# A fixed order for the first layer's drain, its memory attention and its attention loads, a new order at the entry, and other rooms for merged rows

## The chip, the cores and the metric

The kernel runs on one core of a Trainium2 chip. The metric is the device time of one execution in microseconds (us), lower is better. Times are medians of several runs; the profile is one execution of the same program, taken by the hardware profiler.

## The reference

Two layers of a decoder trunk work on 1024 tokens of width 1024, in float32. The first layer is dilated sliding-window attention, the second a gated linear recurrence; both also attend into 256 memory tokens. Only the first layer is touched. Cut to what matters:

```python
h = rms_norm(x, norm_gain[0])
cols = h @ w_in_a                      # q, k, v of 3 groups x 8 heads, memory queries, gate
mix = dilated_mixer(...)               # groups (window, dilation) = (128,1), (512,4), (2048,16)
    # per group: s = q k^T, masked softmax, o = p v; out also log of the denominator
    # o = sum over groups of softmax(lse)[g] * outs[g]      <- the "merge"
mem_out = memory_cross_attention(...)  # 4 heads: softmax(qm km^T) vm
y = concat([mix, mem_out]) * silu(gate)
x = x + y @ w_out
```

Every large product is done in TensorE passes on a split of the operands in a high and a low part (names ending in hi and lo, or h and l): high times high, low times high, high times low. The attention's own small products, s = q k^T and p v, run in float32 as they are.

## The kernel before, in words

Work is tiled by 128 tokens (NT = 8 tiles) and 128 x 512 results in PSUM, whose pools have few rooms: acc 3, s 2, pt (transposes) 2, po 1. Engines run their own queues in order; the order is set by a scheduler, except inside `pinned(...)`, which ties the instructions of the engines it names (TensorE alone when it names none) to the order in which the program writes them. Weights are loaded by SyncE (L204, into "raw" rooms), split by ScalarE (wh, L174 or L221) and VectorE (wl), some pieces ahead: `load_piece` issues a load, `split_piece` splits, `ahead(n)` does both until n pieces are ready.

The parts that the change touches come in this order:

- **Entry** (L1238 to L1297). Token tiles come in pairs j. A tile is scaled on VectorE (xt, L891), turned on TensorE (L896, into the two pt rooms), copied by ScalarE as the high part hhi and as r (L174), and VectorE makes the low part hlo (L910). Sums of a pair, s3, s2 and s4 (`x_sum`, L925), are split by `x_split`: ScalarE makes the high part (L174), GpSimd the low part (L931). In between, TensorE has gate matmuls (L1181 to L1183).
- **Drain of the projections** (L1375 to L1381). The last steps of the big projection are followed by eight steps k = 1 to 8 that finish heads on the other engines: turned heads are copied out of pt by ScalarE (L1113). TensorE runs 12 items of `memory_steps` in each, gate matmuls L591 at this point. Ahead of k = 3 and k = 4, `mem_turn` turns one tile of memory rows (16 transposes, L346, pt rooms; high and low part by ScalarE and VectorE, s3hi L174 and s3lo L324).
- **Memory attention** (L1466 to L1514). A pipeline over m = 0 to NT + 5: project memory queries (m < NT), norm them, turn them (L363), scores (L429 to L431), softmax on ScalarE and VectorE, turn (L458), values (L472 to L474, into po). In the last six steps the projection is over and the table `under` gives TensorE matmuls of a gate slice (L591; one slice has 48) to run between. Slices 0 to 3 of this gate are `MG0 = (0, 1)` and `MG1 = (2, 3)`; slice 1 is used up here.
- **Attention** (L1516 to L1661). Twelve heads in the order (2,0), (1,0), (2,1), (1,1), (0,0), (2,2), (1,2), (0,1), (2,3), (1,3), (0,2), (0,3), written (group, pair of heads); each has 8 steps m. A step gives scores of m (L1543), a turn of m - 2 (L1557) and values of m - 3 (L1570). Groups 1 and 2 write their results by ScalarE into a room of the pool "spill" (3 rooms, os) and from there to the scratch o_scr (`spill`, L1584 to L1592). Group 0 reads those back (og, L1528, two rooms a group), weighs them on GpSimd (L1612, L1613), and `merge` (L1617) adds its own part on VectorE (L1622) into a spill room and stores it. kT, qT and vv of the heads to come are loaded into two sets of rooms, one load a step. In group 2's heads each step also runs 3 matmuls L591 of slices 2 and 3. The attention is pinned on TensorE alone: SyncE's order is the scheduler's.

After the attention the kernel's order is the same in both versions.

## Time and profile before

| what | value |
|---|---|
| runs of the kernel | 2059.63, 2057.74, 2058.79 us; median 2058.79 us |
| the profiled execution's own time | 2058.84 us |
| its span in the profile | 2057.0 us, so 1.84 us lie around it |
| instructions | 29832, of them 10641 matmuls |
| TensorE (PE) busy | 2026.7 us (99%), 30.3 us idle |
| VectorE (DVE), ScalarE (ACT), GpSimd (POOL) busy | 1276.9, 887.1, 569.1 us |

In the profile PE is TensorE, PEld its weight loads, DVE VectorE, ACT ScalarE, POOL GpSimd and SP SyncE, which here issues DMA. L12 is line 12 of the kernel. A timeline row gives the start, the duration, engine, line, operation, `out<-in` and, in brackets, how long the engine had been idle before and what ended that. "granted clock" or PEclk is the share of TensorE's clock that was let through. The engine that is never idle sets the time, and that is TensorE: a change can only save what TensorE waits, or time that it runs slowed.

### The profile page before, as it was taken

The page shows a single profiled execution, that of the slowest core. Times are in us where ns is not written, and L with a number is a line of the kernel's source. Part 1 is how long each engine was busy: PE and PEld are TensorE (multiplying, and loading weights), DVE is VectorE, ACT ScalarE, POOL GpSimd, SP SyncE. Part 2 cuts the span into 40 slices and gives each one's busy share as a digit, 9 for nine tenths or more (in the row PEclk, how much of TensorE's full clock was granted, in tenths as well). Part 3 has the DMA queues.
Part 4 walks back from the last instruction along what each step waited for, and adds up shares of the span by engine and source line. Part 5 has one row for each costly group of instructions (what it writes and reads, how often), then busy time and mean ns, then how long its engine had stood idle before and what let it go on. Part 6 is the DMA issues. An engine that isn't in the chain of part 4 may idle for free.

```text
span 2057.0 us, 29832 instructions
## 1 busy us (share of the span) xinstructions
PE 2026.7 (99%) x10641; PEld 1720.2 (84%) x10641; DVE 1276.9 (62%) x2540; ACT 887.1 (43%) x1678; POOL 569.1 (28%) x690
## 2 busy tenths in 40 slices
PE   7999999999999999999999999999999999999999
PEld 6888888888888887888898888888888888888887
DVE  7745866736767356555567454484554888886543
ACT  6435555633554344546667332253364332232220
POOL 4105765703755046121123200070031000000221
PEclk9999999999999999999999999999999999999999
DMA  6445989553544426617998474524354111213643
GB/s 228 133 134 103 92 143 132 110 169 89 116 124 135 151 73 183 186 36 275 319 326 283 145 255 154 175 72 142 116 176 139 40 44 50 79 37 103 235 133 113
DMA packets 434339, 295.59 MB, mean 144 GB/s; under 512 B 221952, under 2 KB 350224, under 8 KB 434192
## 3 DMA queue, kind: packets, MB, share of 16 engines
q1 hardware_dynamic: 420992, 276.91, 48.1%
q10 hardware_dynamic: 13200, 16.78, 2.2%
q8 instruction: 85, 1.39, 0.3%
q14 instruction: 62, 0.51, 0.1%
HBM read 202.28 MB, written 91.36 MB: 143 GB/s over the span
## 4 chain that ended last, share of the span: by engine, by line
PE 50%; DMA 2%; ACT 1%; DVE 0%; issue 0%; POOL 0%; SPq 0%; ACTq 0%; DVEq 0%
PE acc L662 4%; PE acc L663 4%; PE acc L664 4%; PE acc L558 4%; PE acc L556 4%; PE acc L557 4%; PE s L1543 2%; PE acc L1997 2%; PE s L2142 2%; PE pt L2142 2%; PE acc L294 1%; PE acc L293 1%; PE acc L292 1%; PE pt L1557 1%; PE po L1570 1%; PE acc L1570 1%
## 5 line engine op out<-in xcount | busy, mean ns | idle before, releaser
L174 ACT ACTIVATE wh<-raw 128x1024 fp32r<-128x1024 f32 x207 | 217.2, 1054 | 185.0 <-PE acc L557 59.6
L975 DVE TENSOR_TENSOR wl<-raw,wh 128x1024 fp32r<-128x1024 f32 x136 | 169.2, 1244 | 120.0 <-ACT wh L174 119.4
L1089 POOL TENSOR_TENSOR rr<-rv,nhalf 128x4 f32<-128x4 f32 x96 | 121.5, 1266 | 391.5 <-DVE rv L1087 391.4
L183 POOL TENSOR_TENSOR rr<-rv,nhalf 128x4 f32<-128x4 f32 (+1 forms) x46 | 42.7, 930 | 608.2 <-DVE rv L181 581.8
L662 PE MATMUL acc<-wh,yhi 128*128 128x512 f32 x360 | 142.7, 399 | 0.5 <-ACT yhi L174 0.5
L1044 PE MATMUL acc<-wh,hhi 128*128 128x512 f32 x360 | 141.3, 393 | 0.0
L663 PE MATMUL acc<-wl,yhi 128*128 128x512 f32 x360 | 141.1, 392 | 0.0
L664 PE MATMUL acc<-wh,ylo 128*128 128x512 f32 x360 | 140.2, 394 | 0.0
L1046 PE MATMUL acc<-wh,hlo 128*128 128x512 f32 x360 | 140.2, 390 | 0.0
L1045 PE MATMUL acc<-wl,hhi 128*128 128x512 f32 x360 | 140.1, 389 | 0.0
L556 PE MATMUL acc<-hhi,wh 128*128 128x512 f32 x320 | 128.7, 402 | 0.0
L557 PE MATMUL acc<-hlo,wh 128*128 128x512 f32 x320 | 127.5, 399 | 0.0
L558 PE MATMUL acc<-hhi,wl 128*128 128x512 f32 x320 | 127.4, 398 | 0.0
L236 DVE TENSOR_TENSOR wl<-raw,wh 128x1024 fp32r<-128x1024 f32 x62 | 76.5, 1239 | 67.9 <-ACT wh L174 62.5
L979 DVE TENSOR_TENSOR raw<-raw 128x1024 f32<-128x1024 f32 x76 | 96.5, 1278 | 20.1 <-DMA raw<-in_w_in_a_dram 19.8
L1548 ACT ACTIVATE pa<-pa,st 128x128 f32<-128x128 f32 (+1 forms) x192 | 84.7, 443 | 45.9 <-DVE st L1546 45.4
L1546 DVE CUSTOM_DVE_ANT_0 pa<-s,masks 128x128 f32<-128x128 f32 (+1 forms) x192 | 59.6, 348 | 44.7 <-PE pt L1557 22.6
L674 DVE TENSOR_TENSOR x<-x,acc 128x512 f32<-128x512 f32 x62 | 42.2, 685 | 71.6 <-PE acc L664 71.5
L1543 PE MATMUL s<-kT,qT 128*128 128x128 f32 (+1 forms) x384 | 78.2, 326 | 1.9 <-DVE st L1546 1.1
L662 PEld LDWEIGHTS acc<-wh,yhi 128*128 128x128 f32 x360 | 67.7, 188 | 14.1 <-ACT yhi L174 0.8
L1046 PEld LDWEIGHTS acc<-wh,hlo 128*128 128x128 f32 x360 | 67.6, 188 | 14.2
L664 PEld LDWEIGHTS acc<-wh,ylo 128*128 128x128 f32 x360 | 67.6, 188 | 13.9
(477 smaller groups left out, 5685.4 us busy)
## 6 DMA issues: line engine op xcount, KB each, us to landing
raw<-in_w_in_a_dram SPq DMA_DIRECT2D x109, 512.0 KB, 4.3
raw<-in_w_in_b_dram SPq DMA_DIRECT2D x43, 512.0 KB, 3.9
qk_scr<-m SPq DMA_DIRECT2D x48, 256.0 KB, 3.9
kT<-qk_scr SPq DMA_DIRECT2D x24, 512.0 KB, 5.8
qT<-qk_scr SPq DMA_DIRECT2D x24, 512.0 KB, 7.3
vv<-v_scr SPq DMA_DIRECT2D x24, 512.0 KB, 5.5
o_scr<-os SPq DMA_DIRECT2D x96, 128.0 KB, 5.1
og<-o_scr SPq DMA_DIRECT2D x32, 256.0 KB, 4.8
```

What stands on the lines that cost most here:

```text
L174: A.activation(dst, src, AF.Copy)
L556: T.matmul(ps[:], wh[:, k, :], mh, start=k == 0, stop=False)
L557: T.matmul(ps[:], wh[:, k, :], ml, start=False, stop=False)
L558: T.matmul(ps[:], wl[:, k, :], mh, start=False, stop=k == 7)
L662: T.matmul(pss[ch][:], hi[:, k, :], wh[:, j, :], start=first and k == 0, stop=False)
L663: T.matmul(pss[ch][:], hi[:, k, :], wl[:, j, :], start=False, stop=False)
L664: T.matmul(pss[ch][:], lo[:, k, :], wh[:, j, :], start=False, stop=end and k == 3)
L975: V.tensor_tensor(lo[:], source(n, h), hi.bitcast(F32), op=OP.subtract)
L1044: T.matmul(flat, hi, wh, start=kt == 0 and p in (0, 1, 5), stop=False, **on)
L1045: T.matmul(flat, hi, wl, start=False, stop=False, **on)
L1046: T.matmul(flat, lo, wh, start=False, stop=kt == 3, **on)
L1089: G.tensor_tensor(r[:], sd[:], nhalf[:, :4], op=OP.pow)
```

## The change

- Entry, j = 0 only: the three `x_split` now come behind the copies and low part of the next tile (`x_high`, `x_keep`, `x_low` of tile 2) in place of ahead of them.
- Drain: `mem_turn(0)` comes behind step 3 (before: ahead of it), `mem_turn(1)` ahead of the fifth gate matmul of step 4 (before: ahead of step 4). A Tanh of one column (`A.activation(small.tile(...), nhalf[:, 0:1], AF.Tanh)`) is put ahead of step 1.
- Memory attention: slices 1, 2 and 3 form one stream, `cover`. `under` gives it 66 matmuls (before 48), and the attention's 32 steps of group 2 get the other 78: 2 each in the first 18, 3 each in the last 14 (before 3 in each). Weight pieces are loaded and split at written places, and the loads of the first head (`first_heads`) come one in each half step in place of all at once.
- Attention: SyncE is pinned too, so that loads and stores stand as the program writes them. `merge` takes every other room from the pool "gs" (2 rooms) and so has five in all with "spill". A weight piece is loaded and split at (1, 0) too (before: at odd pairs only).

```diff
                 x_sum(j, "s3")
                 x_sum(j, "s2")
-                x_split(j, "s3")
-                x_split(j, "s2")
-                if a_ and not j:
+                if j:
+                    x_split(j, "s3")
+                    x_split(j, "s2")
+                else:
                     x_scale(a_)
                 x_sum(j, "s4")
-                x_split(j, "s4")
+                if j:
+                    x_split(j, "s4")
...
                         x_low(a_, kh)
+                    if not j:
+                        for n in ("s3", "s2", "s4"):
+                            x_split(j, n)
...
         for k in range(1, BEHIND + 3):
             with pinned():
-                if k in (3, 4):
-                    mts.append(mem_turn(k - 3))
-                for _ in range(96 // (BEHIND + 2)):
+                if k == 1:
+                    A.activation(small.tile([128, 1], F32, name="ss1")[:], nhalf[:, 0:1], AF.Tanh)
+                for j in range(96 // (BEHIND + 2)):
+                    if (k, j) == (4, 4):
+                        mts.append(mem_turn(1))
                     next(ahead_of)
                 step(LAST + k, lambda: pieces(LAST + k))
+                if k == 3:
+                    mts.append(mem_turn(0))
...
-            cover = gate_mem_steps(MG0[1])
+            def fillers():
+                for i in MG0[1:] + MG1:
+                    yield from gate_mem_steps(i, False)
+
+            cover, first_heads = fillers(), fetch(0)
...
-            under = {NT: (8, 8), NT + 1: (5, 5), NT + 2: (4, 4), NT + 3: (3, 3), NT + 4: (2, 2), NT + 5: (2, 2)}
+            under = {NT: (8, 8), NT + 1: (5, 5), NT + 2: (4, 4), NT + 3: (5, 5), NT + 4: (6, 6), NT + 5: (5, 5)}
...
-                                if m == NT - 1 and k % 2:
-                                    ahead(1 + k // 2)
+                                if m == NT - 1 and k in (1, 5):
+                                    ahead(1 + k // 4)
+                                    load_piece()
...
+                    if m == 5:
+                        load_piece()
+                        load_piece()
                     half_step(0)
                     if m == NT:
                         del W
-                        ahead(4)
+                    if m in (NT + 1, NT + 3):
+                        ahead((m - NT + 3) // 2)
+                        load_piece()
+                    if m >= NT:
                         with pinned(E.SP):
-                            fetch(0)
+                            next(first_heads, None)
...
-                y = spool.tile([128, 4, 128], F32, name="os")
+                y = (gs if m // 2 % 2 else spool).tile([128, 4, 128], F32, name="os")
...
-                    with pinned():
+                    with pinned(E.PE, E.SP):
                         new = (g, hp, m, *scores(g, hp, m))
                         old = turn_(*scored.pop(0)) if len(scored) > 1 else None
-                        for _ in range(3 if g == 2 else 0):
-                            next(fill, None)
+                        if g == 2:
+                            give = fills[0] // fills[1]
+                            fills[:] = fills[0] - give, fills[1] - 1
+                            for _ in range(give):
+                                next(cover)
...
-                        if g == 1 and hp % 2:
+                        if g == 1 and hp != 2:
```

Three places show what the order of an engine's queue becomes. The first is TensorE in the drain: w_6746 are the rows of a projected head, raw those of the memory. Before:

```order
L591 MATMUL acc<-hhi,wl 128x512
L363 MATMUL pt<-ident,w_6746 128x128 x8
L346 MATMUL pt<-ident,raw 128x128 x8
L591 MATMUL acc<-hhi,wh 128x512
L591 MATMUL acc<-hlo,wh 128x512
```

And now, from the same turn L363 on (seven more gate matmuls L591 stand between the two fences):

```order
L363 MATMUL pt<-ident,w_6746 128x128 x8
L591 MATMUL acc<-hhi,wh 128x512
L591 MATMUL acc<-hlo,wh 128x512
L591 MATMUL acc<-hhi,wl 128x512
L591 MATMUL acc<-hhi,wh 128x512
```

```order
L591 MATMUL acc<-hhi,wl 128x512
L346 MATMUL pt<-ident,raw 128x128 x8
L591 MATMUL acc<-hhi,wh 128x512
L591 MATMUL acc<-hlo,wh 128x512
L591 MATMUL acc<-hhi,wl 128x512
L591 MATMUL acc<-hhi,wh 128x512
L346 MATMUL pt<-ident,raw 128x128 x8
```

The first eight transposes of memory rows moved behind 12 gate matmuls, and the other eight come four matmuls later in place of twelve. At the same place ScalarE's queue changes too: these are the two pieces of the difference around its table load, the first at the norm of the memory rows (L376), the second ahead of the copy L1113 that empties pt.

```order
 L1077 ACTIVATE s<-m_6837 128x512
 L376 ACTIVATE raw,ss_6855<-raw 128x1024
+L1383 ACT_TABLE_LOAD
+L1383 ACTIVATE ss_7157<-nhalf 128x1
 L174 ACTIVATE m_6875<-po 128x512
 L1077 ACTIVATE s<-m_6875 128x512
```

```order
 L1077 ACTIVATE s<-u_6644 128x512
 L221 ACTIVATE wh<-raw,tabs 128x512 x3
-L519 ACT_TABLE_LOAD
 L519 ACTIVATE os<-acc 128x512
 L1113 ACTIVATE w_6746<-pt 128x512 x2
```

The table load moved some twenty instructions earlier. The second place is ScalarE at the entry, where hhi and r belong to the next tile and s3hi, s2hi, s4hi to the sums of the pair:

```order
+L174 ACTIVATE hhi<-pt 128x4x128
+L174 ACTIVATE r_307<-pt 128x512
+L174 ACTIVATE hhi<-pt 128x4x128
+L174 ACTIVATE r_311<-pt 128x512
 L174 ACTIVATE s3hi<-u_282 128x4x128
 L174 ACTIVATE s2hi<-w_284 128x4x128
-L174 ACTIVATE s4hi<-u_291 128x4x128
-L174 ACTIVATE hhi<-pt 128x4x128
-L174 ACTIVATE r_313<-pt 128x512
-L174 ACTIVATE hhi<-pt 128x4x128
-L174 ACTIVATE r_317<-pt 128x512
+L174 ACTIVATE s4hi<-u_287 128x4x128
```

The tile's four copies now stand ahead of the three sums. The third place is SyncE in the attention, in the first head of group 0; og1 and og2 are the results of groups 1 and 2 that are read back, o_scr00 the merged rows that are stored. Before:

```order
L1528 DMA og2_9584<-o_scr20_106 128x2x256
L1624 DMA o_scr00_102<-os_9601 128x256
L1528 DMA og1_9582<-o_scr10_104 128x2x256
L1624 DMA o_scr00_102<-os_9601 128x256
L1528 DMA og2_9648<-o_scr20_106 128x2x256
L1405 DMA kT_9692<-qk_scr10_95 128x1024 x2
L1624 DMA o_scr00_102<-os_9673 128x256
L1528 DMA og1_9646<-o_scr10_104 128x2x256
```

And now:

```order
L1550 DMA og1_9595<-o_scr10_104 128x2x256
L1550 DMA og2_9597<-o_scr20_106 128x2x256
L1646 DMA o_scr00_102<-os_9614 128x256 x2
L1412 DMA qT_9449<-qk_scr01_93 128x2x512
L1550 DMA og1_9659<-o_scr10_104 128x2x256
L1550 DMA og2_9661<-o_scr20_106 128x2x256
L1646 DMA o_scr00_102<-os_9680 128x256 x2
L1414 DMA kT_9699<-qk_scr10_95 128x1024 x2
```

The two reads of a pair now come together and ahead of the store of the pair before it, the stores of a pair come together, and the loads of later heads are spread among them.

More of the change, by code (lines that the diff above doesn't have):

```diff
@@ L1425, in fetch @@
         def fetch(at):
-            for _ in (*fetch_qk(at), *fetch_v(at)):
-                pass
+            yield from fetch_qk(at)
+            yield from fetch_v(at)
         with ExitStack() as sm:
@@ L1505, in trunk_kernel @@
                     half_step(1)
+                    if m >= NT:
+                        with pinned(E.SP):
+                            next(first_heads, None)
                     if m < NT:
@@ L1511, in trunk_kernel @@
                         shown[m - 3] = mem_scores((m - 3) // 2, (m - 3) % 2, qs, km, prob)
-            for _ in cover:
-                pass
         if True:
@@ L1625, in merge @@
                                  y[:, 2 * i:2 * i + 2].rearrange("p h d -> p (h d)"))
-            def fillers():
-                for i in MG1:
-                    yield from gate_mem_steps(i, False)
-            fill = fillers()
+            fills = [48 * (1 + len(MG1)) - sum(map(sum, under.values())), 4 * NT]
             scored, turned, rest = [], [], []
@@ L1659, in trunk_kernel @@
                         turned.append(old)
-            for _ in fill:
+            for _ in cover:
                 pass
```

## The prediction

> **What bounds the kernel now.** I read the page first, then the chain of waits, then the list of what TensorE waits for, and last the timeline at each wait that lies where the change is.
>
> ```profile
> span 2057.0 us, 29832 instructions
> PE 2026.7 (99%) x10641; PEld 1720.2 (84%) x10641; DVE 1276.9 (62%) x2540; ACT 887.1 (43%) x1678; POOL 569.1 (28%) x690
> PE 50%; DMA 2%; ACT 1%; DVE 0%; issue 0%; POOL 0%; SPq 0%; ACTq 0%; DVEq 0%
> ```
>
> TensorE is busy 99% of the span and holds nearly the whole chain that has a name. The change takes no matmul away, so only the 2057.0 - 2026.7 = 30.3 us in which TensorE idles can be saved, and time in which it runs slowed. The list by what TensorE waits for (us in all, times, longest) says where:
>
> ```profile
> PE pt L896 <- DVE xt L891: 8.1, 2, 7.4
> PE po L1570 <- ACT os L174: 3.7, 2, 2.7
> PE pt L346 <- ACT w L1113: 3.4, 1, 3.4
> PE pt L896 <- DVE hlo L910: 2.4, 2, 2.0
> PE po L1570 <- DVE os L1622: 2.3, 1, 2.3
> PE pt L363 <- DVE pml L324: 1.2, 1, 1.2
> PE s L1543 <- DVE st L1546: 1.1, 3, 0.7
> PE po L474 <- DVE pml L324: 0.9, 3, 0.3
> PE s L1543 <- PE po L1570: 0.7, 1, 0.7
> PE po L472 <- ACT pmh L174: 0.7, 1, 0.7
> PE pt L1557 <- ACT pa L1548: 0.4, 1, 0.4
> ```
>
> The first row is the start, where the first tile has not come in; the change doesn't touch it. All others here lie in its four places: entry 2.4; drain 3.4; memory attention 1.2 + 0.9 + 0.7, with the 0.7 of the first score; attention 3.7 + 2.3 + 0.4 + 0.7 + 0.4 = 7.5 (the row L1543 without that 0.7). Sum 2.4 + 3.4 + 3.5 + 7.5 = 16.8 us. That is the most that can go, slowed matmuls aside.
>
> **Drain.** The timeline around the wait:
>
> ```profile
> 800.35 1.93 ACT L221 ACTIVATE wh<-raw,tabs 128x512 fp32r<-128x512 f32 x3
> 802.30 1.28 ACT L519 ACT_TABLE_LOAD   x1
> 803.60 0.60 ACT L519 ACTIVATE os<-acc 128x512 f32<-128x512 f32 x1
> 804.09 1.08 ACT L1113 ACTIVATE w<-pt 128x512 f32<-128x512 f32 x2
> 804.74 1.97 PE L346 MATMUL pt<-ident,raw 128*128 128x128 f32 x8 [3.41 <-ACT w L1113]
> 807.36 0.63 PE L591 MATMUL acc<-hhi,wl 128*128 128x512 f32 x1
> 807.79 0.63 PE L591 MATMUL acc<-hhi,wh 128*128 128x512 f32 x1
> 811.01 0.39 PE L591 MATMUL acc<-hhi,wl 128*128 128x512 f32 x1
> 811.24 0.93 PE L346 MATMUL pt<-ident,raw 128*128 128x128 f32 x7
> ```
>
> Both rooms of pt are full of a turned head. ScalarE empties them with L1113, which stands behind three splits, a table load and L519. The memory rows' transposes are next on TensorE, so it idles from 801.33 to 804.74. Then it runs slowed: gate matmuls follow each other in 0.43 us (807.36, 807.79) where the last comes 0.23 us ahead of the next operation (811.01, 811.24). At 0.23 the twelve matmuls take 2.8 us, and eight transposes at the last row's pace (0.93 for seven) 1.06; from 804.74 to 811.24 are 6.5, so 6.5 - 3.8 = 2.7 us are the price of the slowed clock.
>
> Two edits act here. With the twelve gate matmuls ahead of them, the transposes are reached at 801.33 + 12 x 0.23 = 804.1. With the table load gone from this place, L519 runs at 802.30, and L1113 is through at 802.30 + 0.49 (803.60 to 804.09) + 1.08 = 803.9. So the wait is covered. The order alone would leave 804.7 - 804.1 = 0.6 of it, the table load alone 3.4 - 1.3 = 2.1. The table load costs 1.28 us elsewhere, at a place where ScalarE later waits for VectorE:
>
> ```profile
> 776.41 0.60 ACT L1077 ACTIVATE s<-w 128x512 f32<-128x512 f32 x1 [3.64 <-DVE w L1068]
> ```
>
> It takes 1.28 of these 3.64 idle us, so I cost it at nothing; without that cover it would be 1.28. What is late next: the second eight transposes come only four matmuls (0.9 us) behind the first and need both rooms again, which ScalarE and VectorE empty in two copies of 0.6 and two subtractions of 0.7; I charge 0.6 (0 to 0.8). Gain 3.4 + 2.7 - 0.6 = **5.5** (4.0 to 6.1).
>
> At this place a page of the Trainium skill has a rule. TensorE: Matmul & The Clock Gate, Part 1, says that the array falls to half clock after an idle window of about 3.4 us and comes back after about as long a busy one. The row of 3.41 us and half pace behind it agrees; worked out from the page, as an estimate, the slowed stretch would cost half of 3.4, some 1.7 us, and the gain would be 4.5; the rows give 2.7, and the sum goes by the rows.
>
> **Entry.** The rows of VectorE, GpSimd and TensorE:
>
> ```profile
> 20.59 0.69 DVE L925 TENSOR_TENSOR w<-m,r 128x512 f32<-128x512 f32 x1
> 21.42 2.20 POOL L931 TENSOR_TENSOR s3lo<-u,s3hi 128x512 fp32r<-128x512 f32 x1 [0.34 <-ACT s3hi L174]
> 22.39 1.77 DVE L925 TENSOR_TENSOR u<-r,w 128x512 f32<-128x512 f32 x1
> 24.09 2.31 DVE L891 SCALAR_TENSOR_TENSOR xt<-xt,rr,gain 128x1024 f32<-128x1024 f32 x1
> 27.05 1.25 PE L896 MATMUL pt<-ident,xt 128*128 128x128 f32 x8 [1.97 <-DVE hlo L910]
> 31.51 1.28 DVE L891 SCALAR_TENSOR_TENSOR xt<-xt,rr,gain 128x1024 f32<-128x1024 f32 x1
> 39.23 1.26 PE L896 MATMUL pt<-ident,xt 128*128 128x128 f32 x8 [0.47 <-DVE hlo L910]
> ```
>
> While GpSimd splits, the same VectorE operation takes 1.77 in place of 0.69 and the scaling 2.31 in place of 1.28: the two keep each other out. That delays hlo, and TensorE waits 1.97. With the splits behind the copies this wait goes. But the splits' work is only moved: ScalarE has its three copies of the sums ahead of the next tile's. Laying out the queues by hand with these durations, I get the scaling now at 31.51 about 0.7 earlier, not 1.97; TensorE, 1.97 early, then waits longer at 39.23, about 1.7 in place of 0.47. Net **0.7** (0, all given back at the later tile, to 2.4, both waits gone).
>
> **Memory attention.** Its waits and the pace of a gate matmul:
>
> ```profile
> 929.30 0.66 PE L363 MATMUL pt<-ident,qn 128*128 128x128 f32 x4 [1.24 <-DVE pml L324]
> 931.46 0.40 PE L591 MATMUL acc<-hhi,wl 128*128 128x512 f32 x1
> 931.69 0.39 PE L591 MATMUL acc<-hhi,wh 128*128 128x512 f32 x1
> 957.62 0.68 PE L1543 MATMUL s<-kT,qT 128*128 128x128 f32 x4 [0.71 <-DVE st L1546]
> ```
>
> The 18 more matmuls of `under` are 18 x 0.23 = 4.1 us, put into the last three steps, where the small waits stand (0.9 + 0.7 of L472 and L474). They cover those and the first score's 0.71, since the softmax that is waited for no longer stands at the end of an empty queue: 2.3, of which I take **1.8** (0.5 to 2.3). The wait at 929.30 lies ahead of them and stays: the splits of weights that the code puts later are put by the scheduler on ScalarE and VectorE where they were, all but one. So "split later" is worth nothing here, from 0 to 1.2. The matmuls are moved, not added: the attention is 4.1 us shorter in work.
>
> **Attention.** Its transfers and two long waits, in windows of 20 us (TensorE, weight loads, VectorE, ScalarE, GpSimd busy; granted clock, DMA share, GB/s), and two pieces of the chain:
>
> ```profile
> 1020.00:1040.00 20.00, 17.25 (x120) 15.85 (x119) 10.11 (x54) 10.34 (x38) 12.96 (x12) 0.91 1.02 347
> 1040.00:1060.00 20.00, 20.00 (x152) 18.74 (x151) 14.27 (x70) 15.32 (x59) 0.04 (x1) 1.00 1.02 337
> ```
>
> ```profile
> 1012.82 3.25 SPq L1403 DMA_DIRECT2D kT<-qk_scr  x2
> 1017.66 6.88 DMA o_scr<-os
> 1025.21 1.57 PE L1570 MATMUL po<-vv,pts 128*128 128x128 f32 x8 [2.75 <-ACT os L174]
> 1080.30 8.34 DMA og<-o_scr
> ```
>
> At 1025.21 TensorE waits for po; ScalarE could not copy it, because no spill room was free; the room waited for a store of 6.88 us, which SyncE had issued late, behind kT loads (3.25 us for two). The clock falls: 0.91 of 20 us, or 1.8 us, lost on top of 2.75. At 1092 it is the read-back og, 8.34 us. The page named above would not let the clock fall after 2.75 us; the 0.91 shows that it does, and I keep the row.
>
> The change gives merges two more rooms and puts stores between single loads. I take the first loss as gone, 2.75 + 1.8 = 4.5, and the second (2.3) as staying, because og has two rooms a group as before and now stands ahead of the merges' stores on SyncE. Against it goes cover: a head of group 2 that loses 8 x 0.23 = 1.8 us of gate matmuls gives less time to the transfers; I charge half, 0.9. Net **3.6**, from a loss of 4.1 (transfers set the pace, and what moved out comes back as waiting) to 9.3 (all 7.5 and 1.8).
>
> **Sum.** 5.5 + 0.7 + 1.8 + 3.6 = 11.6 against the profiled execution's 2058.84 (span 2057.0 and 1.84 around it), which is the median of the three runs, 2058.79, to 0.05. 2058.8 - 11.6 = **2047.2**.
>
> **Rivals.**
>
> *Transfers pace the attention.* The DMA share is 1.0 there, for it; against it, TensorE is busy all 20 us of 1040 to 1060 at the same share, so loads run ahead of need. Then the moved 4.1 us return as waits and the attention's own stay: 2058.8 - 5.5 - 0.7 - 1.8 + 4.1 = 2054.9.
>
> A page of the Trainium skill speaks for this rival: DMA: Bandwidth & Descriptors, Where 436 GB/s comes from, gives a limit of about 358 GB/s for transfers to and from HBM per core. The row at 347 is close to it; no run here shows yet whether it is a limit.
>
> *All attention waits go.* Five rooms and spread loads clear og as well: 2058.8 - 5.5 - 0.7 - 1.8 - 9.3 = 2041.5. For it: the merge's stores at least no longer share rooms with the next head's spills.
>
> *The drain stays.* If the second eight transposes wait as long as the first did now, at 3.4 + 2.7, the drain's gain is nothing: 2047.2 + 5.5 = 2052.7. Against it: L1113 has 1.28 less ahead of it.
>
> *Slower: reads block SyncE.* In program order a read-back waits at the head of SyncE's queue for its room, and behind it the merges' stores, qT and kT. If each of pairs 2 and 3 of the four group-0 heads then costs what 1025.21 did (4.5), eight such cost 36 in place of 9.3: 2058.8 - 5.5 - 0.7 - 1.8 + 27 = 2078. It decides for slower from the point where the eight average (9.3 + 8.0) / 8 = 2.2 us. For it: the queue as shown; against it: a read-back frees within one merge, two steps, and the loads behind it are for heads that come later.
>
> *The change does not do what it says* is a part of the forecast: the later splits.
>
> **How the numbers follow.** Forecast 0.63, transfers pace 0.17, all waits go 0.08, drain stays 0.06, slower 0.06. The range is 2040 to 2055.5: it holds all but the slower case and the tails of the terms, some 0.15. A measurement of this kernel can tell about 0.2%, 4.1 us, from no change, so faster is below 2054.7. The forecast, "all go" and "drain stays" lie below it, and of the transfers' case half: 0.63 + 0.08 + 0.06 + 0.08 = 0.85; within 0.2% its other half, 0.09; slower 0.06.
>
> **What would show it.** In the changed profile: no wait above 1 us at L346 and gate matmuls at 0.23 us behind it; the table load on a line of its own while ScalarE is free; no 1.97 at the entry's second L896 but about 1.7 where 0.47 stands; no waits at L472 and L474; the attention's waits by L1570 below 4 us in all and no window there with a clock below 1. Wrong would be: waits of over 2 us at L1570 for os or og in several group-0 heads, SyncE's issues of og standing for many us, or TensorE's idle time above 25 us.

## The result, and the profile after

The changed kernel takes 2053.28 us (median of 13 runs, 2050.29 to 2057.25) against 2059.63 us (13 runs beside them, 2055.31 to 2063.53): the ratio is 0.9969, with a 95% interval of 0.996 to 0.9978. So it is faster, by 6.4 us (0.3%), inside the range, and by little more than half of the 11.6 us that were forecast. A second set of 11 runs gave 2054.42 us and 0.9977 (0.9969 to 0.9986).

The page of the changed kernel:

```profile
span 2052.1 us, 29806 instructions
PE 2024.2 (99%) x10641; PEld 1715.9 (84%) x10641; DVE 1279.5 (62%) x2540; ACT 884.1 (43%) x1679; POOL 566.2 (28%) x690
PE 45%; DMA 3%; DVE 2%; POOL 1%; ACT 1%; issue 1%; SPq 0%; ACTq 0%; DVEq 0%; POOLq 0%
```

The span is 4.9 us shorter. TensorE idles 2052.1 - 2024.2 = 27.9 us (before 30.3), and its busy time fell by 2.5 us: less of it ran at a slowed clock, as the windows below show. What it waits for now, some rows of 0.7 us and less left out:

```profile
PE pt L896 <- DVE xt L891: 9.0, 3, 7.3
PE po L1592 <- DVE os L1644: 3.2, 3, 1.8
PE s L1565 <- DVE st L1568: 1.9, 3, 1.3
PE pt L363 <- DVE pml L324: 1.4, 1, 1.4
PE pt L896 <- DVE hlo L910: 1.4, 2, 1.0
PE pt L1579 <- ACT pa L1570: 1.1, 3, 0.4
PE acc L389 <- DVE qn L357: 0.9, 1, 0.9
PE po L474 <- DVE pml L324: 0.7, 2, 0.5
PE pt L346 <- DVE s3lo L324: 0.7, 1, 0.7
PE s L1565 <- DVE mM L1629: 0.6, 1, 0.6
```

The waits for os and w on ScalarE are gone. New are waits of the attention for VectorE (L1644 the merge, L1568 the mask and maximum, L1629 the weights), and one at L389 where before there was none.

Sums of waits don't say where time is won, so I followed the same matmul through both profiles: its start in the changed kernel minus its start before, in us. The order on TensorE is the same at these marks. Each row is one profiled execution, the marks are starts before the change: 801.05 (the last matmul of a turn L363 ahead of the drain's wait), 814.96 (the turn L363 behind it), 850 (L389, memory keys and values), 943 (a gate matmul in the memory attention), 1146.0 (L294, just behind the attention) and 1300.

| kernel | 801 | 815 | 850 | 943 | 1146 | 1300 | median, us |
|---|---|---|---|---|---|---|---|
| changed | -1.28 | -6.40 | -4.95 | -4.75 | -6.05 | -5.27 | 2053.28 |
| changed, second set | -0.76 | -6.10 | -3.12 | -3.07 | -5.95 | -5.80 | 2054.42 |
| turns alone | +0.59 | -4.22 | -4.24 | -4.09 | -4.09 | -3.77 | 2054.78 |
| table load alone | +0.01 | -2.26 | -2.22 | -2.67 | -0.18 | -0.17 | 2056.69 |
| entry alone | -0.89 | -2.02 | -2.06 | -1.88 | -2.17 | -1.50 | 2059.70 |
| order alone | +0.61 | -0.28 | -0.23 | -0.80 | -2.53 | -2.25 | 2059.41 |
| gains early | -0.26 | -5.68 | -5.69 | -5.50 | -8.94 | -8.42 | 2050.59 |
| SyncE free | -0.74 | -6.30 | -3.36 | -3.82 | +1.11 | +1.26 | 2058.06 |
| three rooms | -1.01 | -6.49 | -5.59 | -5.51 | -8.88 | -7.54 | 2051.24 |
| attention as before | -0.76 | -6.00 | -3.61 | -3.38 | -2.46 | -2.42 | 2056.59 |
| reads swapped | -0.97 | -6.42 | -4.76 | -4.95 | -8.68 | -8.27 | 2050.20 |
| gains and swap | -0.88 | -6.42 | -6.42 | -6.37 | -9.24 | -8.70 | 2049.67 |
| gains, swap, early reads | -0.37 | -6.36 | -6.39 | -6.39 | -14.13 | -13.59 | 2044.91 |

The first row reads: entry 1.3 us won, drain 5.1 won, then 1.5 given back behind it; the end of the memory attention and the attention together win 1.3; 0.8 is lost behind them, which was not followed further. Two things stand out against the forecast: a loss between 815 and 850, where I had no term, and an attention that wins nearly nothing.

The drain in the changed kernel:

```profile
768.90 1.28 ACT L1383 ACT_TABLE_LOAD   x1
799.75 1.93 ACT L221 ACTIVATE wh<-raw,tabs 128x512 fp32r<-128x512 f32 x3
801.59 0.58 ACT L519 ACTIVATE os<-acc 128x512 f32<-128x512 f32 x1
802.07 1.06 ACT L1113 ACTIVATE w<-pt 128x512 f32<-128x512 f32 x2
802.70 1.14 PE L346 MATMUL pt<-ident,raw 128*128 128x128 f32 x8
805.50 1.26 PE L346 MATMUL pt<-ident,raw 128*128 128x128 f32 x8 [0.73 <-DVE s3lo L324]
```

The table load is early, L1113 follows L519 at once, the first eight transposes wait for nothing, and the second eight wait 0.73 us (0.6 was charged). Behind that, on the same engines:

```profile
810.52 0.37 SPq L204 DMA_DIRECT2D w<-in_w_mem_kv_dram  x1
810.95 0.93 SPq L1462 DMA_DIRECT2D mgt<-in_mem_gain_t_dram  x2
814.31 0.16 DVE L1464 TENSOR_TENSOR mgk<-mgt 128x1 f32<-128x1 f32 x1 [6.19 <-DMA mgt<-in_mem_gain_t_dram]
820.47 0.72 ACT L221 ACTIVATE wh<-raw,tabs 128x512 fp32r<-128x512 f32 x1 [6.83 <-DMA raw<-in_w_mem_kv_dram]
834.67 0.50 PE L389 MATMUL acc<-wh,s3hi 128*128 128x512 f32 x1 [0.85 <-DVE qn L357]
```

VectorE stands 6.19 us for two loads of 1 KB, the gains of the memory keys; SyncE issues them only at 810.95, behind a weight load (810.52) that had waited 5.4 us for a store. Before the change they stood ahead of that load. While VectorE stands it splits no weights, no raw room comes free, ScalarE waits 6.83 us for the next piece, and TensorE waits at 834.67.

In the attention the same rows as before, in windows of 20 us:

```profile
1020.00:1040.00 20.00, 18.18 (x125) 16.80 (x124) 14.57 (x68) 9.94 (x40) 10.20 (x10) 0.91 0.99 322
1040.00:1060.00 20.00, 20.00 (x150) 18.67 (x150) 14.19 (x70) 16.18 (x59) 0.00 (x0) 1.00 0.96 296
1120.00:1140.00 20.00, 19.05 (x117) 16.60 (x116) 18.24 (x71) 12.14 (x41) 15.29 (x15) 1.00 0.63 196
```

The slowed clock of 1020 to 1040 is still there, and in 1120 to 1140, the last 20 us of the attention, VectorE is busy 18.24 of 20 us. The last two heads, both of group 0, begin at 1097; this is where the first merge of theirs stands:

```profile
1105.55 1.01 SPq L1550 DMA_DIRECT2D og<-o_scr  x2
1112.77 1.27 POOL L1635 TENSOR_TENSOR og<-og,og 128x512 f32<-128x512 f32 x1
1114.07 1.12 DVE L1644 SCALAR_TENSOR_TENSOR os<-acc,mw,og 128x128 f32<-128x128 f32 x4 [2.94 <-POOL og L1635]
1115.22 0.82 DVE L1623 TENSOR_TENSOR mw<-mM,st 128x12 f32<-128x12 f32 x1
1116.88 1.10 PE L1565 MATMUL s<-kT,qT 128*128 128x256 f32 x4 [1.27 <-DVE st L1568]
```

The read og is issued at 1105.55, GpSimd is through at 1114.0, and VectorE has stood 2.94 us in the merge with the next scores queued behind it. Heads tell where the attention won and lost; starts against the kernel before, in us:

| head | changed | second set | three rooms | SyncE free | order alone | gains and swap | gains, swap, early reads |
|---|---|---|---|---|---|---|---|
| (1,0) | -5.08 | -3.43 | -5.87 | -4.16 | -0.16 | -6.71 | -6.75 |
| (0,0) | -7.24 | -5.58 | -8.03 | -4.00 | -1.73 | -8.87 | -8.90 |
| (2,2) | -11.18 | -9.52 | -11.96 | -8.68 | -6.41 | -12.81 | -12.83 |
| (1,2) | -7.96 | -8.00 | -12.31 | +0.06 | -4.92 | -13.10 | -11.78 |
| (0,2) | -9.44 | -10.07 | -11.92 | +1.11 | -4.55 | -14.35 | -14.49 |
| (0,3) | -9.20 | -9.99 | -11.40 | +1.11 | -3.80 | -13.18 | -14.43 |
| behind it, 1146 | -6.05 | -5.95 | -8.88 | +1.11 | -2.53 | -9.24 | -14.13 |

In the changed kernel head (0,0) wins 3.9 us, the loss at 1025 that the forecast spoke of. The kernel with SyncE free wins 4.7 there too and loses it elsewhere, so this head shows where a wait went and not what cleared it. Head (2,2) behind it gives 3.2 back (1.5 in the second set), and the last head 3.2 (4.0).

### The profile page after: what moved, and what is told of

It is laid out like the page before. It is cut to its first block, busy times and chain, and to the rows that moved or that the text cites. A ratio compares the mean times of both kernels' runs of the same rounds, so it can differ in the third digit from the quotient of the medians.

```text
span 2052.1 us, 29806 instructions
## 1 busy us (share of the span) xinstructions
PE 2024.2 (99%) x10641; PEld 1715.9 (84%) x10641; DVE 1279.5 (62%) x2540; ACT 884.1 (43%) x1679; POOL 566.2 (28%) x690
## 4 chain that ended last, share of the span: by engine, by line
PE 45%; DMA 3%; DVE 2%; POOL 1%; ACT 1%; issue 1%; SPq 0%; ACTq 0%; DVEq 0%; POOLq 0%
PE acc L662 4%; PE acc L664 4%; PE acc L663 4%; PE acc L558 3%; PE acc L556 3%; PE acc L557 3%; PE acc L2018 2%; PE s L2163 2%; PE pt L2163 2%; PE acc L293 1%; PE acc L294 1%; PE acc L292 1%; DMA og<-o_scr 1%; PE s L1565 1%; PE acc L1046 1%; PE acc L1045 1%
## 5 line engine op out<-in xcount | busy, mean ns | idle before, releaser
L1568 DVE CUSTOM_DVE_ANT_0 pa<-s,masks 128x128 f32<-128x128 f32 (+1 forms) x192 | 59.5, 347 | 39.2 <-PE s L1565 17.7
```

## The experiments

Theory when they were planned: the drain and the entry are as forecast; behind the drain the late gain loads cost about 1.6 us; in the attention the order on SyncE wins and the late, paired reads lose. Rivals: the table load is to blame behind the drain; the five rooms carry the attention; transfers pace it.

**Turns alone.** On the kernel before, only the places of `mem_turn`:

```diff
-                if k in (3, 4):
-                    mts.append(mem_turn(k - 3))
-                for _ in range(96 // (BEHIND + 2)):
+                for j in range(96 // (BEHIND + 2)):
+                    if (k, j) == (4, 4):
+                        mts.append(mem_turn(1))
                     next(ahead_of)
                 step(LAST + k, lambda: pieces(LAST + k))
+                if k == 3:
+                    mts.append(mem_turn(0))
```

> The kernel before with the new places of the two memory turns alone, the table load left where it was. Forecast's theory: the wait at L346 falls from 3.41 us to about 0.6 and the clock stays up, so this alone carries most of the drain's gain up to the turns: 4 to 5 us by the next turn L363. Theory formed from the profile after: the turns' new place also puts the two small loads of memory gains (mgt) behind a weight load that waits for a store; VectorE then stands behind the gains for about 6 us, and 1.3 to 1.8 us are given back before the memory attention, so by its waits of L363 on DVE some 2.5 to 3.5 us are left, and the time is that much below the kernel before. Rival: the give-back belongs to the table load, then none of it is seen here and 4 to 5 us are left.

2054.78 us, ratio 0.998 (0.997 to 0.9989). Waits of the drain:

```profile
PE pt L346 <- ACT w L1113: 0.9, 1, 0.9
```

0.9 where 0.6 was forecast; 4.8 us are won up to 815, and the time is 4.2 us below the kernel before. But nothing is given back by 850, though the gain loads stand late here too (VectorE stands 5.27 us for them). So the late loads alone don't cost; they seem to set a time that TensorE runs into only when it is further ahead than the 4.2 us of this kernel. That part of the expectation missed.

**Table load alone.** On the kernel before, only the early Tanh:

```diff
             with pinned():
+                if k == 1:
+                    A.activation(small.tile([128, 1], F32, name="ss1")[:], nhalf[:, 0:1], AF.Tanh)
                 if k in (3, 4):
```

> The kernel before with the early Tanh alone, the memory turns left where they were. Forecast's theory: the wait at L346 falls by the table load's 1.28 us, from 3.41 to about 2.1 us; whether the clock falls behind a wait of 2.1 us is open (a wait of 2.75 us did it, one of 2.33 did not): 1.3 us gained if it falls as before, up to 4 if it does not. The loads of memory gains keep their place ahead of the weight load, so nothing is given back behind it. Rival: the table load only moves, to a place where somebody waits for ScalarE: then no gain at all.

2056.69 us, ratio 0.9989 (0.998 to 0.9998).

```profile
PE pt L346 <- ACT w L1113: 2.3, 1, 2.3
```

And its window from 800 to 820:

```profile
800.00:820.00 20.00, 17.70 (x92) 14.99 (x91) 11.72 (x21) 10.76 (x20) 6.26 (x11) 0.91 0.65 199
```

The wait is 2.3 (2.1 forecast), the clock falls all the same (0.91, against 0.83 in the kernel before), and 2.3 us are won by 815. Alone the two edits win 4.8 and 2.3, together 5.1 to 6.0 (nine profiles): they overlap, as two ways to the same wait must. About 1 us of each of these figures seems to belong to the one profile that they are taken against: entry alone and order alone, whose drain is that of the kernel before, have a clock of 0.91 there as well, and win 1.1 and 0.9 us from 801 to 815 without any edit in it.

**Entry alone.** On the kernel before, only the hunk of the entry shown above (the three `x_split` behind `x_low`).

> The kernel before with the entry's new order alone. Forecast: the wait of 1.97 us at the second turn L896 goes and the later one grows, net 0.7 us. By the profile after it is 1.26 us at 48 us of the span, constant from there to the drain; the time is 1.3 us below the kernel before. Rival: part of the 1.26 is the start of this one execution (its first waits differ by some tenths), then 0.7.

2059.7 us, ratio 1.0 (0.9991 to 1.001): nothing that the times can tell. In the profiles, the eight other kernels with the new entry and this one stand at -0.3 to -1.3 by 801, and the three other kernels with the old entry at 0.0 to +0.6. So it is worth about 1 us, and one execution differs from the next there by as much as that. In the two kernels at +0.6 the clock fell behind the entry's wait, which the last section comes back to.

**Gains early.** On the changed kernel, the two small loads at the program's start, into a tile that was only padding:

```diff
-    small.tile([128, 32], F32, name="left", bufs=1)
+    left = small.tile([128, 32], F32, name="left", bufs=1)
...
         ahead_of = memory_steps()
+        mgts = left[:, 0:4]
+        for l in range(2):
+            Y.dma_start(mgts[:, 2 * l:2 * l + 2], mem_gain_t[l])
...
-                    gt = ipool.tile([128, 2], F32, name=f"mgt{l}")
-                    Y.dma_start(gt[:], mem_gain_t[l])
+                    gt = mgts[:, 2 * l:2 * l + 2]
```

> The changed kernel with the two loads of memory gains at the program's start in place of in the drain. Theory: VectorE's wait of 6.19 us for them in the drain goes, weight rooms come free earlier, loads follow, and the wait of 0.85 us at L389 and the slowed stretch around it go: the 1.6 us given back there return, so 1.3 to 1.8 us below the changed kernel, seen already at the first turn L363 of the memory attention. Rival: the loads of weights are paced by their own chain of rooms, then the wait for the gains only changes its name and at most 0.3 us come.

2050.59 us, ratio 0.996 (0.9948 to 0.9973), 2.7 us below the changed kernel where 1.3 to 1.8 were expected. What VectorE waits for between 800 and 842, first in the changed kernel, then here:

```profile
DVE wl L233 <- ACT wh L221: 9.2, 4, 3.1
DVE mgk L1464 <- DMA mgt<-in_mem_gain_t_dram: 6.4, 2, 6.2
```

```profile
DVE wl L233 <- ACT wh L221: 11.9, 7, 3.3
DVE qn L357 <- POOL rr L183: 1.1, 2, 0.9
```

The wait for the gains is gone, and so is the loss: -5.68 at 815, -5.69 at 850. All six profiles with the new turns, the early table load and late gains lose 0.9 to 3.0 us there, all three with early gains nothing. The side effect of the turns' new place is shown.

**SyncE free, three rooms, and both.** On the changed kernel, one or both lines undone:

```diff
-                    with pinned(E.PE, E.SP):
+                    with pinned():
...
-                y = (gs if m // 2 % 2 else spool).tile([128, 4, 128], F32, name="os")
+                y = spool.tile([128, 4, 128], F32, name="os")
```

> The changed kernel with SyncE's order in the attention left to the scheduler, five rooms kept. Theory: with SyncE in program order the read of group 1 stands ahead of that of group 2, and both wait for the merge of two pairs before (SyncE waits 17 us on VectorE's merge there, 12 us on GpSimd's addition before the change); in the last two group-0 heads, which follow each other, that loop is longer than TensorE's two steps and gives back 3 to 4 us between 1112 and 1146 us. Without the program order this give-back falls below 1.5 us, and what was gained in the attention before that, 4.5 us, falls too, since stores stand behind loads again: the time is within 2 us of the changed kernel. Rival of the forecast (the order is what clears the long waits): the time is 3 to 4 us above the changed kernel, with no give-back to lose.

> The changed kernel with merges in the spill pool alone, three rooms as before, SyncE in program order. Forecast's theory: the two more rooms are what clears the wait of 2.75 us with its slowed 1.7; without them 2 to 4.5 us come back. Rival: program order puts the stores out early enough, and rooms are not short; then within 1 us of the changed kernel.

> The changed kernel with both edits of the attention undone (SyncE free, three rooms); entry, drain, and the memory attention with its 18 more matmuls stay. It shows what the moved matmuls do alone. Forecast: 1.8 us gained at the start of the attention; the attention's waits stay at about 7.5 us with 1.7 of slowed clock, so 2 to 4 us above the changed kernel. Rival (transfers pace the attention): the 4.1 us moved out come back as waits, and it is 4 to 6 us above the changed kernel. Third: the two edits bring nothing together, then it is within 1 us of it.

SyncE free: 2058.06 us, ratio 0.9993 (0.9984 to 1.0002), 4.8 above the changed kernel. Its waits in the attention:

```profile
PE po L1592 <- DVE os L1644: 6.9, 1, 6.9
PE s L1565 <- DVE st L1568: 2.9, 1, 2.9
PE po L1592 <- ACT os L174: 2.6, 1, 2.6
```

With five rooms, but without the order, the wait for os on ScalarE is back at 2.6, and behind a read-back, which took 8.54 us from 1025.86, TensorE waits 6.9. Three rooms with the order: 2051.24 us, ratio 0.9957 (0.9944 to 0.9969); no wait for os on ScalarE is in its list. So on the changed kernel the order clears that wait and the rooms bring nothing; the forecast had it the other way. Attention as before: 2056.59 us, ratio 0.9991 (0.9981 to 1.0002), 3.3 above the changed kernel. It keeps the entry, the drain and the 18 moved matmuls, and from 943 to 1146 it loses 0.9 us, so the moved matmuls bring little by themselves. The last head gives nothing back in the kernel with SyncE free (+1.11 to +1.11), as the theory had it; that the time would stay within 2 us was wrong, and the rival's 3 to 4 us were nearer.

**Reads swapped.** On the changed kernel, group 2 read and weighed first:

```diff
-                for g in (1, 2):
+                for g in (2, 1):
                     o = ap_.tile([128, 2, 256], F32, name=f"og{g}")
...
-                    got.append(o[:].rearrange("p m (h d) -> p (m h) d", h=2))
+                    got.insert(0, o[:].rearrange("p m (h d) -> p (m h) d", h=2))
...
-                    for g in (1, 2):
+                    for g in (2, 1):
                         G.tensor_tensor(og[g - 1], og[g - 1], wg(g), op=OP.mult)
```

> The changed kernel with the read of group 2 ahead of that of group 1, and GpSimd weighing group 2 first. Theory of the loop of read rooms: group 2's room is free once GpSimd has added (before the merge), so its read no longer waits for the merge and its multiplication of 1.02 us leaves the loop merge, read, two multiplications, addition, merge; over eight pairs in two rooms that is 8 x 1.02 / 2 = 4.1 us at most, so the give-back between 1112 and 1146 us, 3.2 us in the changed kernel, falls below 1.5 and the time by 1.5 to 3 us. Rival: VectorE is slowed there by GpSimd (operations with two inputs in SBUF) and the order of the reads changes nothing: within 1 us.

2050.2 us, ratio 0.9954 (0.9941 to 0.9967), 3 us below the changed kernel; but the last head still loses 3.4 us (-12.11 to -8.68), so it isn't the loop of rooms that costs there. What it won lies in the heads before, where executions differ (the last paragraph of this section), so the theory of the loop is not shown.

**The changed kernel again, and the combinations.** The changed kernel without any edit; then both edits above, and on top of these the first two reads of a group-0 head in the head before it:

```diff
+                        after = heads[at + 1] if at + 1 < len(heads) else (2, 0)
+                        if g == 1 and after[0] == 0 and m in (5, 7):
+                            others(after[1], m - 5)
-                        if g == 0 and m % 2:
+                        if g == 0 and m % 2 and (m > 3 or heads[at - 1][0] == 0):
                             others(hp, m - 1)
```

> The changed kernel itself, beside the next three on the same chip. If the median of 2053.3 us is its level, it comes within 1.5 us of that, 5 to 8 us below the kernel before; its heads in the attention may begin up to 2 us apart from the first profile, since the transfers there do not land alike in two executions. If it comes at 2050 to 2051.5 us, then neither the three rooms nor the swapped reads brought anything, and the three kernels that ran at 2050 to 2051 us are the changed kernel's equals.

> The changed kernel with both the early gains and the swapped reads. If the two effects are real and lie in different places, their differences to the changed kernel add: 1.5 us behind the drain (no wait at L389) and whatever the swap brings (it did not remove the loss in the last head), so 2 to 4.5 us below the changed kernel. Rival: the gains' 1.5 us are given back in the attention, whose end is set by transfers; then it is within 1 us of the swapped reads alone.

> As the kernel with early gains and swapped reads, and the reads of the first two pairs of a group-0 head, where its rooms are free, already in the last steps of the head before. Theory: in the last two heads VectorE stands 3.2 us in the first merge, because its read was issued only four steps before and takes 5 us, and GpSimd 3.3 more; that stands in front of the next scores and costs TensorE 2.9 us there, which goes: the last two heads lose less than 2 us (3.2 to 5.6 before) and the time falls by 1.5 to 3 us. Rival: VectorE is slowed by GpSimd in those steps (0.17 us operations take 0.8 to 1.0), which does not change: within 1 us of the kernel without early reads.

Again: 2054.42 us, ratio 0.9977 (0.9969 to 0.9986), 1.1 from the first median, so that is its level. Gains and swap: 2049.67 us, 0.9961 (0.9948 to 0.9975), which is 3.6 to 4.8 us below the changed kernel, but only 0.9 below early gains alone and 0.5 below swapped reads alone; so the times don't show that the two add up. With early reads: 2044.91 us, 0.994 (0.9928 to 0.9953), 14.3 us below the kernel before it, 8.4 to 9.5 below the changed kernel and 4.8 below gains and swap, where 1.5 to 3 were expected. All that TensorE waits for in its attention, and the last 40 us of that attention, which ends here at 1131.9:

```profile
PE po L1594 <- DVE os L1646: 1.0, 2, 0.6
PE pt L1581 <- ACT pa L1572: 0.9, 3, 0.3
PE s L1567 <- DVE st L1570: 0.9, 3, 0.4
PE s L1567 <- DVE mw L1625: 0.6, 1, 0.6
```

```profile
1092.00:1112.00 20.00, 20.00 (x152) 18.79 (x151) 11.88 (x64) 15.04 (x53) 6.55 (x6) 1.00 0.93 278
1112.00:1132.00 20.00, 20.00 (x126) 17.64 (x125) 11.42 (x62) 11.59 (x39) 12.18 (x12) 1.00 0.56 160
```

TensorE is busy all of these 40 us, the last two heads lose 0.4 us (5.1 without early reads), and VectorE is busy 11.42 us in the last 20 us, where the changed kernel had 18.24. The small operations that took 0.82 us beside GpSimd take 0.17 again, all but one (0.85 at 1115.00), since GpSimd now works at another time. The merges still wait for GpSimd (1.22 us at 1109.52, 2.01 at 1120.61), but TensorE no longer waits behind them. The edit also changed more than the reads. GpSimd's order is the scheduler's, and in these heads it now has the products of two pairs (L1636, two each) and then their two additions (L1637), where they alternated before:

```profile
1102.88 2.04 POOL L1636 TENSOR_TENSOR og<-og,mw 128x512 f32<-128x512 f32 x2 [26.25 <-DVE mw L1633]
1106.20 2.04 POOL L1636 TENSOR_TENSOR og<-og,mw 128x512 f32<-128x512 f32 x2 [1.28 <-DMA og<-o_scr]
1108.20 2.51 POOL L1637 TENSOR_TENSOR og<-og,og 128x512 f32<-128x512 f32 x2
```

So the loss of the last heads goes with this edit; how much of that is the earlier read and how much the new order of merges is not separated.

**Order alone.** On the kernel before, only `pinned(E.PE, E.SP)` in the attention.

> The kernel before with SyncE pinned in the attention, and nothing else: three rooms, 3 matmuls in each step of group 2, no matmul moved. If the order alone carries the attention's gain, heads 5 to 10 begin 3 to 6 us earlier against the first head than in the kernel before, the last two give 2 to 4 us back, and the time is 1.5 to 3.5 us below it. Forecast's rival theory: the moved matmuls carry it through the waits that they cover at the start, 1.8 us; then the order alone gives less than 1.5 us.

2059.41 us, ratio 1.0 (0.9991 to 1.0009). The profile has head (0,0) winning 4.7 us (-1.73 to -6.41) and 3.9 given back from there to 1146; 1.7 are left between 943 and 1146, and the times show nothing. One long wait stands in what was given back: a merge waits 5.26 us for a store, VectorE's masks of the scores stand behind it until 1071.9, and TensorE idles 2.47 us ("issue" means that the profile names no releaser).

```profile
1070.15 1.12 DVE L1622 SCALAR_TENSOR_TENSOR os<-acc,mw,og 128x128 f32<-128x128 f32 x4 [5.26 <-DMA o_scr<-os]
1072.06 1.19 PE L1543 MATMUL s<-kT,qT 128*128 128x128 f32 x4 [2.47 <-issue]
```

The clock falls there too (0.91 from 1060 to 1080). Whether three rooms are short in this kernel, or in this execution alone, is not shown. So neither the order alone nor the moved matmuls alone (attention as before) win much. The changed kernel has both and wins 1.3 and 2.9 in its two profiles, two others with both and the old reads 3.4 each, the two with swapped reads 3.7 and 2.9: the effects seem to help each other, but single executions scatter here by up to 2.5 us (table load alone, whose attention is that of the kernel before, loses 2.5 there, entry alone wins 0.3), so I don't give that a number, and why they should is open.

## Why the prediction was right or wrong

The time lies in the range, which the attention's term (-4.1 to 9.3) had made wide. Term by term the first profile has 1.3 (entry) + 5.1 (drain) - 1.5 and - 0.2 (behind it) + 2.6 (memory attention) - 1.3 (attention) - 0.8 (behind that) = 5.2 us by 1300. Of the rivals, "the drain stays" comes nearest in number (2052.7), but its mechanism did not happen, so that is chance. Two of the signs named for being wrong did show: TensorE idles 27.9 us, above the 25, and a window of the attention has a clock of 0.91.

**Entry**, forecast 0.7: right in kind, and worth about 1 us. Of the wait of 1.97 there is 0.33 left, and the late one grew from 0.47 to 1.03, not to 1.7:

```profile
25.85 0.66 PE L896 MATMUL pt<-ident,xt 128*128 128x128 f32 x4 [0.33 <-DVE hlo L910]
37.99 1.25 PE L896 MATMUL pt<-ident,xt 128*128 128x128 f32 x8 [1.03 <-DVE hlo L910]
```

A further 1.04 at the turn before is in the first profile alone; the second set and entry alone don't have it.

**Drain**, forecast 5.5 and 0.6 for the second turns: measured 5.1 to 6.0 by 815, with 0.73 at the second turns. Against the two other profiles with the old drain (entry alone and order alone) it is about 1 us less, so some of the hit is luck of the one profile that the forecast was read from. The two single effects (0.6 and 2.1 left) came out at 0.9 and 2.3. What failed is that the step ended there. The moved turns also moved two loads of 1 KB on SyncE, behind a weight load that waits for a store, and VectorE's queue stood behind them. That cost 0.9 to 3.0 us at 834, 30 us later. The order of SyncE showed it; I had followed TensorE and ScalarE there, and not the queue that issues the loads.

**Memory attention**, forecast 1.8: measured 2.6. By head (1,0), where 8 of the 18 moved matmuls are back (10 x 0.23 = 2.3 still ahead of it), the shift went from -4.75 to -5.08, so 0.3 + 2.3 = 2.6 were won; the second set gives 2.6 too. The wait at 929.30 stayed, as forecast (1.4 now). The waits at L472 and at the first score went; at L474 0.7 of 0.9 stayed, against the forecast. The 2.6 are above the 2.3 that these waits could give, and where the rest was won is not shown.

**Attention**, forecast 3.6: measured 1.3 - 2.6 = -1.3 in the first profile and 2.9 - 2.6 = 0.3 in the second. This is the term that made the gain half of what was forecast, and its step failed twice. The waits changed their names and not their sum: 7.5 us before, about 7.2 and 7.9 in the two profiles. "The change gives merges two more rooms and puts stores between single loads. I take the first loss as gone": the waits for os on ScalarE did go, but by the order, not by the rooms. And "against it goes cover ... I charge half, 0.9": the charge was taken from the wrong place. What the rows of the last heads show is a read-back that is issued four steps before its merge in program order; with 5 us for the read and 3.3 for GpSimd that is late, and VectorE stands in the merge ahead of the next scores. The rival of reads that block had the right object, and SyncE does stand at them:

```profile
SPq L1550 <- DVE os L1644: 17.1, 9, 3.4
```

But it stood 13.3 us at them before the change too, and what TensorE waits for in these heads is VectorE, not the loads or stores behind the reads. With the reads ahead, and the order of merges that came with that, the time fell by 4.8 us against gains and swap. What the cover costs was not measured.

**Transfers pace the attention** falls: the kernel with early reads moves the same bytes, waits 3.4 us in its whole attention and loses 0.4 us in the last two heads. Its window from 1060 to 1080 carries 378 GB/s, so neither the 347 of the prediction's row nor the 358 set beside it is a limit here.

**The change does not do what it says**: the later splits were worth nothing that shows (the wait at 929.30 stayed), and on the changed kernel the two more rooms weren't either, which I had not seen.

## What to carry to other kernels

When a step is moved, list what it does to the order of each queue, the smallest transfers too: a load of 1 KB behind a load that waits for a store held a whole engine for 6 us. Putting a queue in program order can win where a scheduler's guess puts stores behind loads (about 5 us on the changed kernel, nothing on the kernel before), but every read then starts where it is written; so try to write the reads as early as their rooms allow. And when two waits of an order are removed, look at where each kernel stands some heads later before adding the gains: here 1.5 us were given back some 30 us after they were won, and 3 to 4 us some 100 us after.

## What the runs showed of the hardware that I had not expected

The clock's fall is not decided by the length of the wait alone. At the entry's turn at 27 us the four kernels with the old order wait 1.95 to 1.97 us. In two of them (turns alone, shown first, and order alone) the clock falls behind that wait, in the other two (the kernel before, shown second, and table load alone) it doesn't:

```profile
20.00:40.00 20.00, 17.41 (x81) 14.02 (x80) 18.00 (x22) 12.95 (x24) 14.13 (x10) 0.91 0.69 229
20.00:40.00 20.00, 17.56 (x90) 13.82 (x89) 17.86 (x22) 12.85 (x25) 14.78 (x11) 1.00 0.74 248
```

In the attention a wait of 1.82 us (at 1026.71 in the changed kernel) brought it down, and one of 2.61 (at 1088.49 in attention as before) did not. A slowed stretch is 3.4 us at half clock or a multiple: in the changed kernel the clock is 0.50 from 1027.08 to 1030.49, in the kernel before from 803.93 to 810.76. That costs 1.7 or 3.4 us; a window of 20 us then shows 0.91 or 0.83. The drain's wait of 3.41 us had the double stretch, waits of 3.7 and 3.9 us at the same place in entry alone and order alone the single one. The Trainium skill, TensorE: Matmul & The Clock Gate, Part 1, says that the activity window runs freely, and gives about 3.4 us of idle as what it takes; the first agrees with waits of one length that end differently, the second does not, since 1.82 us were enough here.

The same program's transfers don't land alike: the first read og of head (0,0) took 5.30 us in one profile of the changed kernel and 4.50 in the other, with the same queues. But head (2,2), which lost 3.2 us in the one and 1.5 in the other, differs by the clock: the wait in it is 1.82 and 1.73 us, and only the first brought a slowed stretch of 1.7 us.

And those of VectorE's operations on 12 columns that have two inputs, 0.17 us alone, take up to 1.0 while GpSimd works (0.82 in the row at 1115.22); the reductions and reciprocals, with one input, keep their 0.15 to 0.18. The Trainium skill, SBUF — State Buffer, Who interferes with whom, has the rule that a VectorE operation with two inputs in SBUF and a GpSimd one that reads SBUF shut each other out, and these rows agree. So a queue of small operations can become the bound where its share of the whole span (62%) looks harmless.
